# The last pair of output rows reordered, and the scaling of the causal pool put directly behind a reciprocal in both attentions

## The chip, the cores and the metric

The kernel runs on one core of a Trainium2 chip. The metric is the device time of one execution in microseconds (us). Five engines work side by side: TensorE (PE, with its weight load as PEld), VectorE (DVE), ScalarE (ACT), GpSimd (POOL) and SyncE (SP). Each runs its own instructions in the order in which they were written down for it; semaphores tie them together. In this kernel SP issues most of the DMAs, in its own order; a few are issued by ACT.

## The reference

One layer of a decoder trunk with 2048 positions and width 1024, all in float32:

```python
shift, scale, gate = split(silu(c) @ w_ada + b_ada)
u = x * (1 + scale) + shift
q, k, v, a_gate, p_in, p_gate, m_a, m_p = split(u @ w_in)
a = sliding_window_attention(q, k, v, sinks, bias) * silu(a_gate)     # window 128, 16 heads, 2 kv heads
a = a @ w_attn_proj
p = group_linear(causal_pool(p_in), w_pool_mix)                       # windows 2, 4, 8, 16
p = (p * pool_scale) * silu(p_gate)
p = p @ w_pool_proj
y = (sigmoid(m_a) * a + sigmoid(m_p) * p) @ w_out * (1 + gate)
x = layer_norm(alpha * x + y, ln_gain, ln_bias)
```

The causal pool of window w is the mean of the last w positions less the position itself. The part of it that the change touches is written in the kernel as `sum * (1/w) - value`, and then times the gate.

## The kernel before, in words

**Products.** Every product of two float32 blocks is made of three matmul passes over a high and a low half (`hi`, `lo`), so it stays accurate to float32. A block product of 256 rows by 1024 columns is a "quad" of a Strassen-like scheme: seven products, called B11, T1, T2, B21, T3, B22 and T4, of 12 matmuls of 128x512 each (`product`). Four of them are sums that several outputs share, so a few additions on DVE lie between them. In the profile an operand of a product is `set_B`, `set_T` or, in the last rows, `t4h`/`t4l`, its other operand is `w_set`; `mm` and `lg` are PSUM banks.

**Stages.** The sequence is worked in two halves of 1024 positions. For each half the gates are projected first, then the attention runs, and after both halves come the attention projection, the pool projection and the merge, and last `w_out` with the LayerNorm, in pairs of rows of 128 positions (`finish_pairs`, `out_quad`). The first attention takes from 256.3 to 584.8 us of the profiled execution, the second from 827.0 to 1157.8 us.

**An attention.** `attention` runs 67 iterations of about 4.9 us. An iteration issues, in this order, the scores of one block on PE (`lg<-kk,qs`), the transposes of an earlier block (`pt<-ident,L`), a reciprocal of sums on DVE (`sm<-sm`), then `close()`, the additions of the outputs `o` on DVE behind a copy on ACT (`o<-pv`), the scaling of probabilities `L<-L,sm` and the split of the transposed block (`pth` on ACT, `ptl` on DVE), the exponentials (`L<-L,nm` on ACT), five or six steps of three matmuls of other products (`filling`, 13 quads in all that have nothing to do with this block), the value matmuls (`pv<-pth,vv` and `pv<-ptl,vv`), and last `run_coming`, which runs whatever was queued for this iteration with `later`.

**What the fill products leave.** Their results go one of three ways. `take_p` makes the causal sums on POOL (`vb` to `nxt` to `fin`, as many additions as the window has powers of two), then, an iteration or two on, scales on DVE (`fin<-fin,...`), multiplies by the gate on POOL (`fin<-fin,pg`), and one iteration later sends the result to DRAM with a DMA on SP (`pin_B<-fin`). This happens 32 times, 16 in each half. `take_gate` copies a result to `raw` on ACT and sends it away with a DMA on SP (`ma_d<-raw`, `mp_d<-raw`); the tag `raw` has one buffer, so the next copy to it waits until the DMA before has landed. `seed` copies a bank on ACT (`mm<-mm`) that T2 of the next quad is accumulated onto. `split` prepares an operand: POOL adds the two blocks (`W<-W`), ACT casts the high half and POOL or DVE makes the low one (`w_set`); its blocks `W` and `A` are loaded by SP. In SP's order the loads of the next quad and the DMA of `raw` stand behind a `pin_B<-fin` at several places.

**`close()`.** The list `closing` holds additions `c + p5` of a quad (L948ff). It is emptied after the reciprocal of each iteration and ahead of T3 and T4.

**The last rows.** In `finish_pairs` a quad's T2, B21, T3, B22, T4 follow each other; T4 is accumulated onto the bank of T3 (`lg`). `consume` (L709) adds a product to the row held in `wide`, `last_stats` takes statistics of a half (L680), `last_norm` aggregates them (L685), adds epsilon (L686), makes the inverse root on POOL (L687, a power), multiplies by the gain (L688), and only when both rows 14 and 15 are done multiplies by the inverse root and adds the bias, by halves of 512 (L695), each followed by its DMA (L696). Most operations here are recorded with the line of a helper, L57.

The order in which `dve`, `pool`, `act`, `sp` and `pe` get their instructions is the program's own (`Ordered`); what is written with `nc.vector` may be moved by the scheduler.

Of the kernel before, what the change touches and what calls it, by code (L numbers as in the profile page):

```python
# [15 lines left out]
ALU = mybir.AluOpType  # L16
# [3 lines left out]
P = 128  # L20
D = 1024
S = 2048
KT = D // P
CH = 512
# [8 lines left out]
ALPHA = 2.0 ** 0.25  # L33
EPS = 1e-5
POOL_W = (2, 4, 8, 16)
# [25 lines left out]
def kernel(  # L61
# [22 lines left out]
    nc = tc.nc  # L84
# [15 lines left out]
    carry = cp.tile([P, KT, 16], F32, name="carry")  # L100
# [24 lines left out]
    def cols(t, n):  # L125
        return t[:, n * CH : (n + 1) * CH]
# [286 lines left out]
    def finish_pairs(ph, grp, opened, tick):  # L413

        lasts = []
        for q in grp:
            hi, lo = (ph.c(n, F32R) for n in ("t4h", "t4l"))
            nc.scalar.copy(hi, q.a22)
            low(nc.vector, lo, q.a22, hi)
            lasts.append((hi, lo))  # L420

        def begin(x):
            q, (a, b, _, _) = grp[x], opened[x]
            c, p5 = bank("lg"), ph.p("p5")
            nc.scalar.copy(c, a)
            nc.scalar.copy(p5, b)
            w = pair_split(ph, q.second())[::-1]
            q.late()
            return a, b, c, p5, w

        got = begin(0)
        for x, q in enumerate(grp):
            a, b, c, p5, w = got
            product(c, w[1], "T2")
            tick()
            w3 = pair_split(ph, q.third())[::-1]
            nc.vector.tensor_tensor(b, c, p5, ALU.add)
            product(a, w[0], "B21")
            tick()
            q.consume(ph, 0, 0, a)  # L440
            product(c, w3[1], "T3")
            tick()
            nc.vector.tensor_tensor(p5, c, p5, ALU.add)
            q.consume(ph, 1, 1, p5)
            product(b, w3[0], "B22")
            if x + 1 < len(grp):
                got = begin(x + 1)
            tick()
            q.consume(ph, 0, 1, b)
            product(c, lasts[x], "T4")  # L450
            tick()
            q.consume(ph, 1, 0, c)

# [189 lines left out]
    def norm_row(ph, row, z):  # L643
# [32 lines left out]
        for at, f in ((1, squares), (2, power), (3, scale), (3, store)):  # L676
            defer(at, f)

    def last_stats(row, n, zn):
        nc.vector.bn_stats(carry[:, row - 12, 6 * n : 6 * n + 6], zn)  # L680

    def last_norm(row, z):

        st, mv, rs = (carry[:, row - 12, a:b] for a, b in ((0, 12), (12, 14), (14, 15)))
        nc.vector.bn_aggr(mv, st)  # L685
        nc.vector.tensor_scalar(rs, mv[:, 1:2], EPS, None, ALU.add)  # L686
        nc.gpsimd.tensor_tensor(rs, rs, mhalf, ALU.pow)  # L687
        nc.vector.scalar_tensor_tensor(z, z, mv[:, 0:1], vec["gain"], ALU.subtract, ALU.mult)  # L688
        ending.append((row, z, rs))
        if row + 1 < S // P:  # L690
            return
        for row, z, rs in ending[::-1]:
            for n, q in enumerate((nc.sync, nc.scalar)):
                zn = cols(z, n)
                nc.vector.scalar_tensor_tensor(zn, zn, rs, cols(vec["lnb"], n), ALU.mult, ALU.add)  # L695
                q.dma_start(out[row * P : (row + 1) * P, n * CH : (n + 1) * CH], zn)  # L696

    ending = []

    def y_row(row):  # L700
        return y_d[row // 8, :, row // 4 % 2, :, row % 4 * P : (row % 4 + 1) * P].rearrange("k p q -> p k q")

    def out_quad(k):
        def consume(ph, mi, n, src):
            row = k + mi
            z, n_done = zs[row]
            zs[row][1] += 1
            zn = cols(z, n)
            nc.vector.scalar_tensor_tensor(zn, zn, ALPHA, src, ALU.mult, ALU.add)  # L709
# [66 lines left out]
    def attention(ph, s, fills, post, opened):  # L776
# [56 lines left out]
        def take_p(m, t, acc):  # L833
            n = max(now_n[0], pool_free[1] + 1, pool_free[0] + 3)
            pool_free[:] = pool_free[1], n
            wait = 1 if POOL_W[m // 2] < 8 else 2
            own = (m % 2, t) == (0, 1)
            x = []

            def first():  # L840
                x.append(ld("pg", gates_d["pg"][s, m, t], 2))
                x.extend(pool_sums(m, t, acc))

            def second():
                pg, p, copied = x
                dve.scalar_tensor_tensor(
                    p, p, 1.0 / POOL_W[m // 2], copied if own else acc, ALU.mult, ALU.subtract
                )
                pool.tensor_tensor(p, p, pg, ALU.mult)
                later(n + wait + 1, lambda: keep_raw(pin_d[s], m, t, p))  # L850

            later(n + wait, second)
            if own:
                free_b[0] = n
            if n == now_n[0]:
                first()
            else:
                later(n, first)
# [86 lines left out]
        closing = []  # L945

        def close():
            while closing:
                x, name = closing.pop()
                _, b, c, p5 = st[x]  # L950
                dve.tensor_tensor(b if name == "T2" else p5, c, p5, ALU.add)

        def filling():
            for i, (x, name) in enumerate(seq):
                begun(i)
                if name in ("T3", "T4"):
# [154 lines left out]
                sp.dma_start(as32(vv[:, 1 + NB :]), v_d[s, :, 1 + NB :])  # L1111
        for _ in fill:
            pass
        run_coming(True)
        result = []
        for x, q in enumerate(post):
# [558 lines left out]
```

## Time and profile before

| | |
|---|---|
| time, median of 3 runs (lowest to highest) | 1681.29 us (1681.26 to 1681.58) |
| profiled execution: its time | 1681.68 us |
| profiled execution: span of the core | 1679.9 us |
| DVE busy | 1208.6 us, 72% |
| ACT busy | 1026.3 us, 61% |
| POOL busy | 949.3 us, 57% |
| granted TensorE clock, mean | 0.997 |

The span is the time from the first to the last recorded instruction; 1.78 us of the profiled execution's own time lie outside it, and that execution took 0.39 us more than the median. In rows of a timeline the first number is the start in us, the second what it took in us, then engine, line, operation, `out<-in`, shape and a count; brackets at the end tell how long the engine had been idle and what ended that. A row of the engine SP tells when the DMA was issued, not when it landed. Several operations of one kind in a row are one row with a count.

### The profile page before, as it was taken

What the parts mean: (1) busy time and instruction counts of PE and PEld (TensorE: products, weight loads), DVE (VectorE), ACT (ScalarE), POOL (GpSimd) and SP (SyncE); (2) the same over time, 40 slices, a digit from 0 to 9 for tenths busy, and PEclk for the clock granted to TensorE, in tenths of its full rate; (3) what the DMA queues carried; (4) which work ended last, traced back from release to release, by engine and by line L of the source; (5) the groups of instructions that cost most, each with busy time, mean ns of one, the idle gap of its engine ahead of it and who ended that gap; (6) DMA issues with size and microseconds to landing.
All of it is one profiled execution on the core that took longest, in us unless ns stands there. A gap on an engine that the chain in (4) does not pass through costs nothing.

```text
span 1679.9 us, 24661 instructions
## 1 busy us (share of the span) xinstructions
PE 1642.9 (98%) x8058; PEld 1382.7 (82%) x8058; DVE 1208.6 (72%) x2156; ACT 1026.3 (61%) x2146; POOL 949.3 (57%) x710
## 2 busy tenths in 40 slices
PE   7999999999999999999999999999999999999997
PEld 6788888888888788888888888888878878878886
DVE  6955656676867867566467677777769896979777
ACT  4754547778778755334577777776647464554452
POOL 3343437585867838773376858597445453423442
PEclk9999999999999999999999999999999999999999
DMA  9688844343543578872432335345968896677443
GB/s 362 209 291 296 204 158 124 99 126 107 176 137 113 188 278 298 312 273 94 154 128 88 126 131 171 118 127 188 330 215 313 274 321 219 227 271 235 155 147 113
DMA packets 185971, 331.56 MB, mean 197 GB/s; under 512 B 18017, under 2 KB 43761, under 8 KB 185841
## 3 DMA queue, kind: packets, MB, share of 16 engines
q1 hardware_dynamic: 182720, 325.72, 56.8%
q10 hardware_dynamic: 3088, 4.23, 1.1%
q8 instruction: 64, 1.05, 0.3%
q14 instruction: 67, 0.54, 0.1%
q0 software_dynamic: 32, 0.02, 0.0%
HBM read 223.77 MB, written 109.28 MB: 198 GB/s over the span
## 4 chain that ended last, share of the span: by engine, by line
PE 80%; DVE 7%; DMA 5%; ACT 3%; issue 2%; POOL 2%; SPq 1%; POOLq 0%; DVEq 0%; ACTq 0%
PE mm L57 51%; PE lg L57 22%; PE pv L57 4%; PE pt L57 4%; DMA head_T<-in_wada_dram 1%; DMA g<-mp_d 1%; DVE w_set L132 1%; DVE L L57 1%; SPq L57 1%; DVE set_T L57 1%; DMA head_B<-in_wada_dram 1%; DVE room L57 1%; DVE w_set L57 0%; DMA g<-ma_d 0%; ACT g L609 0%
## 5 line engine op out<-in xcount | busy, mean ns | idle before, releaser
L57 PE MATMUL mm<-set_B,w_set 128*128 128x512 f32 x2664 | 652.6, 392 | 0.9 <-DVE w_set L57 0.4
L57 PEld LDWEIGHTS mm<-set_B,w_set 128*128 128x128 f32 x2664 | 495.8, 188 | 103.2 <-DVE w_set L57 0.8
L57 PE MATMUL mm<-set_T,w_set 128*128 128x512 f32 x1824 | 453.4, 395 | 2.1 <-DVE mm L57 1.2
L57 PE MATMUL lg<-set_T,w_set 128*128 128x512 f32 x1704 | 411.3, 391 | 7.6 <-ACT w_set L303 2.8
L57 PEld LDWEIGHTS mm<-set_T,w_set 128*128 128x128 f32 x1824 | 336.3, 188 | 70.8 <-DVE mm L57 4.2
L57 PEld LDWEIGHTS lg<-set_T,w_set 128*128 128x128 f32 x1704 | 319.6, 188 | 78.0 <-issue 3.7
L132 DVE TENSOR_TENSOR w_set<-W,w_set 128x1024 fp32r<-128x1024 f32 x137 | 192.5, 1405 | 142.3 <-ACT w_set L303 133.0
L303 ACT CAST w_set<-W 128x1024 fp32r<-128x1024 f32 x137 | 144.0, 1051 | 192.8 <-PE mm L57 148.3
L266 POOL TENSOR_TENSOR W<-W,A 128x512 f32<-128x512 f32 x46 | 73.5, 1598 | 271.6 <-DMA A<-in_win_dram 66.5
L57 POOL TENSOR_TENSOR w_set<-W,w_set 128x512 fp32r<-128x512 f32 x120 | 159.1, 1333 | 110.4 <-ACT w_set L57 108.6
L57 DVE TENSOR_TENSOR o<-pv,o 64x128 f32<-64x128 f32 x256 | 71.9, 281 | 96.8 <-ACT o L57 93.4
L57 POOL TENSOR_TENSOR W<-W 128x512 f32<-128x512 f32 x82 | 111.1, 1368 | 52.8 <-DVE sm L57 25.8
L57 ACT ACTIVATE L<-L,nm 128x257 f32<-128x257 f32 (+1 forms) x256 | 127.1, 498 | 17.8 <-DVE nm L57 8.2
L275 POOL TENSOR_TENSOR W<-W 128x512 f32<-128x512 f32 x46 | 71.9, 1563 | 103.9 <-DVE w_set L132 94.0
L270 POOL TENSOR_TENSOR W<-W 128x512 f32<-128x512 f32 x44 | 80.3, 1828 | 83.1 <-DVE w_set L132 66.7
L57 DVE CUSTOM_DVE_ANT_0 L<-lg,bt,nsink 128x256 f32<-128x256 f32 (+1 forms) x256 | 111.6, 473 | 15.2 <-DMA pg<-pg_d 10.8
L57 ACT CAST w_set<-W 128x512 fp32r<-128x512 f32 (+1 forms) x165 | 101.4, 628 | 24.4 <-POOL W L57 14.5
L57 ACT COPY o<-pv 64x256 f32<-64x256 f32 x128 | 47.3, 369 | 71.3 <-PE pv L57 70.1
L271 POOL TENSOR_TENSOR W<-W 128x512 f32<-128x512 f32 x44 | 69.1, 1570 | 32.4 <-DMA W<-in_win_dram 16.4
L57 ACT ACTIVATE L<-L,sm 128x256 f32<-128x256 f32 (+1 forms) x128 | 64.3, 502 | 36.6 <-DVE sm L57 36.2
L57 DVE TENSOR_TENSOR ptl<-pt,pth 128x512 fp32r<-128x512 f32 (+1 forms) x128 | 85.7, 669 | 1.0 <-ACT pth L57 0.9
L57 POOL TENSOR_TENSOR spare<-spare 128x512 f32<-128x512 f32 x48 | 80.2, 1679 | 8.1 <-ACT spare L57 6.0
(233 smaller groups left out, 2411.6 us busy)
## 6 DMA issues: line engine op xcount, KB each, us to landing
W<-in_win_dram SPq DMA_DIRECT2D x42, 512.0 KB, 5.8
W<-in_win_dram SPq DMA_DIRECT2D x42, 256.0 KB, 4.0
A<-in_win_dram SPq DMA_DIRECT2D x42, 256.0 KB, 4.9
ag_d<-sig SPq DMA_DIRECT2D x32, 256.0 KB, 5.9
pg_d<-sig SPq DMA_DIRECT2D x32, 256.0 KB, 4.4
pg<-pg_d SPq DMA_DIRECT2D x32, 256.0 KB, 3.2
pin_B<-fin SPq DMA_DIRECT2D x32, 256.0 KB, 2.0
ag<-ag_d SPq DMA_DIRECT2D x32, 256.0 KB, 3.1
```

Of the source, the lines that this page charges most:

```text
L57: return lambda *args, **kw: self.tc.keep_in_program_order(op(*args, **kw))
L132: engine.tensor_tensor(dst, src, as32(hi), ALU.subtract)
L266: e.tensor_tensor(self.w[:, 1, :], self.w[:, 2, :], self.a22, ALU.add)
L270: e.tensor_tensor(x[:, 1, :], x[:, 1, :], x[:, 0, :], ALU.subtract)
L271: e.tensor_tensor(x[:, 2, :], x[:, 0, :], x[:, 2, :], ALU.subtract)
L275: e.tensor_tensor(x[:, 3, :], x[:, 3, :], x[:, 1, :], ALU.subtract)
L303: a.copy(by_two(hi), raw)
```

## The change

**In the attentions.** `second` no longer scales and multiplies by itself in `run_coming`. It appends a function (`scaled`) to `closing`, which runs behind the next iteration's reciprocal, or ahead of T3 or T4 if that comes first. The additions `c + p5` now go into the same list, at its front. The DMA of the result stays queued for the same iteration as before.

**In the last pair.** For the last quad alone B22 is computed ahead of T3. T4 goes into the bank that B21 left, from nothing, in place of being accumulated onto T3's bank. The parts of the rows that are known early are added in place (`partly`), so that at the end a plain addition is left. The final scaling of a row is made of two functions (`last_halves`); the first half of row 14 is run ahead of T4, the rest after the last gain operation. The operations of the last two rows are kept in program order.

```diff
@@ finish_pairs
             q.consume(ph, 0, 0, a)
+            last = x + 1 == len(grp)
+            if last:
+                q.consume(ph, 1, 1, p5, True)
+                product(b, w3[0], "B22")
+                tick()
+                q.consume(ph, 0, 1, b)
             product(c, w3[1], "T3")
             tick()
-            nc.vector.tensor_tensor(p5, c, p5, ALU.add)
-            q.consume(ph, 1, 1, p5)
-            product(b, w3[0], "B22")
-            if x + 1 < len(grp):
+            if last:
+                q.consume(ph, 1, 1, c)
+                ending.pop(0)()
+                q.consume(ph, 1, 0, c, True)
+                c = a
+            else:
+                nc.vector.tensor_tensor(p5, c, p5, ALU.add)
+                q.consume(ph, 1, 1, p5)
+                product(b, w3[0], "B22")
                 got = begin(x + 1)
-            tick()
-            q.consume(ph, 0, 1, b)
-            product(c, lasts[x], "T4")
+                tick()
+                q.consume(ph, 0, 1, b)
+            product(c, lasts[x], "T4", last)
             tick()
             q.consume(ph, 1, 0, c)
@@ last_norm
+    def last_halves(row, z, rs):
+
+        def half(n, q):
+            zn = cols(z, n)
+            dve.scalar_tensor_tensor(zn, zn, rs, cols(vec["lnb"], n), ALU.mult, ALU.add)
+            q.dma_start(out[row * P : (row + 1) * P, n * CH : (n + 1) * CH], zn)
+
+        return [lambda n=n, q=q: half(n, q) for n, q in enumerate((nc.sync, nc.scalar))]
...
-        nc.vector.scalar_tensor_tensor(z, z, mv[:, 0:1], vec["gain"], ALU.subtract, ALU.mult)
-        ending.append((row, z, rs))
-        if row + 1 < S // P:
-            return
-        for row, z, rs in ending[::-1]:
-            for n, q in enumerate((nc.sync, nc.scalar)):
-                zn = cols(z, n)
-                nc.vector.scalar_tensor_tensor(zn, zn, rs, cols(vec["lnb"], n), ALU.mult, ALU.add)
-                q.dma_start(out[row * P : (row + 1) * P, n * CH : (n + 1) * CH], zn)
+        dve.scalar_tensor_tensor(z, z, mv[:, 0:1], vec["gain"], ALU.subtract, ALU.mult)
+        ending.extend(last_halves(row, z, rs))
+        if row + 1 == S // P:
+            for f in ending:
+                f()
@@ out_quad
+        begun = set()
+
+        def consume(ph, mi, n, src, partly=False):
...
+            if (row, n) in begun:
+                e.tensor_tensor(zn, src, zn, ALU.add)
+            else:
+                e.scalar_tensor_tensor(zn, zn, ALPHA, src, ALU.mult, ALU.add)
+            if partly:
+                begun.add((row, n))
+                return
@@ attention, take_p
             def second():
                 pg, p, copied = x
-                dve.scalar_tensor_tensor(
-                    p, p, 1.0 / POOL_W[m // 2], copied if own else acc, ALU.mult, ALU.subtract
-                )
-                pool.tensor_tensor(p, p, pg, ALU.mult)
+
+                def scaled():
+                    dve.scalar_tensor_tensor(
+                        p, p, 1.0 / POOL_W[m // 2], copied if own else acc, ALU.mult, ALU.subtract
+                    )
+                    pool.tensor_tensor(p, p, pg, ALU.mult)
+
+                closing.append(scaled)
                 later(n + wait + 1, lambda: keep_raw(pin_d[s], m, t, p))
@@ attention, close
         def close():
             while closing:
-                x, name = closing.pop()
-                _, b, c, p5 = st[x]
-                dve.tensor_tensor(b if name == "T2" else p5, c, p5, ALU.add)
+                closing.pop(0)()
+
+        def add_up(x, name):
+            _, b, c, p5 = st[x]
+            dve.tensor_tensor(b if name == "T2" else p5, c, p5, ALU.add)
...
-                        closing.append((x, name))
+                        closing.insert(0, lambda x=x, name=name: add_up(x, name))
```

The orders of SP and ACT are the same in both kernels, and PE's differs only in the last pair. POOL's and DVE's change at the 32 places of `take_p`. At 16 of them POOL's multiplication by the gate moves behind what followed it: at eight behind the multiplication of an output `o` by its gate, at two behind a sum `fin<-vb`, at two behind a `w_set`, and at four (the 10th and 14th of each attention, counted from 0) behind the whole set of sums of the next block.

The 14th place of the first attention, on POOL, before (`nxt` and the first `fin` are the sums of the next block, `fin_5779` is the block that is being finished, `pg` its gate, `W` and `w_set` operands of later products, `o` and `ag` an output of the attention and its gate):

```order
L57 TENSOR_TENSOR w_set_5917<-A22_5362,w_set_5917 128x512
L57 TENSOR_TENSOR fin_5779<-fin_5779,pg_5767 128x512
L57 TENSOR_TENSOR nxt_5939<-vb_5935 128x526
L57 TENSOR_TENSOR nxt_5941<-nxt_5939 128x524
L57 TENSOR_TENSOR nxt_5943<-nxt_5941 128x520
L57 TENSOR_TENSOR fin_5945<-nxt_5943 128x512
L57 TENSOR_TENSOR W_5695<-W_5695 128x512 x2
L57 TENSOR_TENSOR w_set_6045<-W_5695,w_set_6045 128x512
L57 TENSOR_TENSOR fin_5945<-fin_5945,pg_5933 128x512
L57 TENSOR_TENSOR o_5812<-o_5812,ag_5876 128x512
```

The same place on POOL now (numbers of the names shift by two):

```order
L57 TENSOR_TENSOR w_set_5917<-A22_5362,w_set_5917 128x512
L57 TENSOR_TENSOR nxt_5937<-vb_5933 128x526
L57 TENSOR_TENSOR nxt_5939<-nxt_5937 128x524
L57 TENSOR_TENSOR nxt_5941<-nxt_5939 128x520
L57 TENSOR_TENSOR fin_5943<-nxt_5941 128x512
L57 TENSOR_TENSOR fin_5779<-fin_5779,pg_5767 128x512
L57 TENSOR_TENSOR W_5695<-W_5695 128x512 x2
L57 TENSOR_TENSOR w_set_6045<-W_5695,w_set_6045 128x512
L57 TENSOR_TENSOR o_5812<-o_5812,ag_5876 128x512
L57 TENSOR_TENSOR fin_5943<-fin_5943,pg_5931 128x512
```

The multiplication `fin_5779<-fin_5779,pg_5767` now stands behind the four sums of the next block, and the next one (`fin_5943,pg`) behind `o_5812`.

SP around the DMA of that block, in the order that holds before and now (`pin0_B21<-fin_5779` is the row `pin_B<-fin` of the profile; `W` and `A22` are loads of a quad's blocks; `raw` is the result of another product):

```order
L57 DMA pg_5931<-pg_d_134 128x512
L57 DMA pin0_B21_120<-fin_5779 128x512
L57 DMA W_6040<-in_win_dram 128x512
L57 DMA A22_6041<-in_win_dram 128x512
L57 DMA W_6040<-in_win_dram 128x2x512
L57 DMA ma_d_135<-raw_6037 128x512
L57 DMA ain0_T1_102<-room1_5857 128x512
```

Nothing moved here: the DMA of `fin_5779` is ahead of three loads and of the DMA that empties `raw`.

DVE at the 15th place, shortly after, as one piece of the difference with the rows around it:

```order
 L57 TENSOR_TENSOR room0_5856<-room0_5856,room1_5857 128x512
-L57 SCALAR_TENSOR_TENSOR fin_5945<-fin_5945,p5_5491 128x512
 L57 RECIPROCAL sm_6026<-sm_6026 128x2
+L57 SCALAR_TENSOR_TENSOR fin_5943<-fin_5943,p5_5491 128x512
 L57 TENSOR_TENSOR o_6079<-pv_6060,o2_6080 64x128 x2
```

The reciprocal now stands ahead of the scaling, as at all 32 places.

DVE at the end of the program before (`wide4` is row 14, `wide5` row 15, `carry` the statistics, `wide0` and `wide1` the gain and the bias):

```order
L688 SCALAR_TENSOR_TENSOR wide4_16248<-wide4_16248,carry_73,wide0_15123 128x1024
L709 SCALAR_TENSOR_TENSOR wide5_16305<-wide5_16305,lg_16296 128x512
L695 SCALAR_TENSOR_TENSOR wide4_16248<-wide4_16248,carry_73,wide1_15125 128x512
L680 BN_STATS carry_73<-wide5_16305 128x6
L695 SCALAR_TENSOR_TENSOR wide4_16248<-wide4_16248,carry_73,wide1_15125 128x512
L685 BN_AGGR carry_73<-carry_73 128x2
L686 TENSOR_SCALAR carry_73<-carry_73 128x1
L688 SCALAR_TENSOR_TENSOR wide5_16305<-wide5_16305,carry_73,wide0_15123 128x1024
L695 SCALAR_TENSOR_TENSOR wide5_16305<-wide5_16305,carry_73,wide1_15125 128x512 x2
```

And now:

```order
L57 SCALAR_TENSOR_TENSOR wide4_16248<-wide4_16248,carry_73,wide0_15123 128x1024
L57 TENSOR_TENSOR wide5_16305<-lg_16296,wide5_16305 128x512
L57 BN_STATS carry_73<-wide5_16305 128x6
L57 SCALAR_TENSOR_TENSOR wide4_16248<-wide4_16248,carry_73,wide1_15125 128x512
L57 SCALAR_TENSOR_TENSOR wide5_16305<-wide5_16305,lg_16296 128x512
L57 TENSOR_TENSOR wide5_16305<-mm_16187,wide5_16305 128x512
L57 BN_STATS carry_73<-wide5_16305 128x6
L57 BN_AGGR carry_73<-carry_73 128x2
L57 TENSOR_SCALAR carry_73<-carry_73 128x1
L57 SCALAR_TENSOR_TENSOR wide5_16305<-wide5_16305,carry_73,wide0_15123 128x1024
L57 SCALAR_TENSOR_TENSOR wide4_16248<-wide4_16248,carry_73,wide1_15125 128x512
L57 SCALAR_TENSOR_TENSOR wide5_16305<-wide5_16305,carry_73,wide1_15125 128x512 x2
```

Before, both halves of row 14 were scaled around the statistics of row 15; now one half is, and the other follows row 15's gain operation. The first half of row 15 is completed by two operations, first from T3's bank (`lg`), then from T4's (`mm`), where it was one.

More of the change, by code (lines that the diff above doesn't have):

```diff
@@ L677, in norm_row @@
             defer(at, f)
+    ending = []
+    def last_halves(row, z, rs):
[4 more added lines that the diff above has]
+        return [lambda n=n, q=q: half(n, q) for n, q in enumerate((nc.sync, nc.scalar))]
     def last_stats(row, n, zn):
-        nc.vector.bn_stats(carry[:, row - 12, 6 * n : 6 * n + 6], zn)
+        dve.bn_stats(carry[:, row - 12, 6 * n : 6 * n + 6], zn)
     def last_norm(row, z):
         st, mv, rs = (carry[:, row - 12, a:b] for a, b in ((0, 12), (12, 14), (14, 15)))
-        nc.vector.bn_aggr(mv, st)
-        nc.vector.tensor_scalar(rs, mv[:, 1:2], EPS, None, ALU.add)
+        dve.bn_aggr(mv, st)
+        dve.tensor_scalar(rs, mv[:, 1:2], EPS, None, ALU.add)
         nc.gpsimd.tensor_tensor(rs, rs, mhalf, ALU.pow)
-        nc.vector.scalar_tensor_tensor(z, z, mv[:, 0:1], vec["gain"], ALU.subtract, ALU.mult)
-        ending.append((row, z, rs))
-        if row + 1 < S // P:
-            return
-        for row, z, rs in ending[::-1]:
-            for n, q in enumerate((nc.sync, nc.scalar)):
-                zn = cols(z, n)
-                nc.vector.scalar_tensor_tensor(zn, zn, rs, cols(vec["lnb"], n), ALU.mult, ALU.add)
-                q.dma_start(out[row * P : (row + 1) * P, n * CH : (n + 1) * CH], zn)
-    ending = []
+        dve.scalar_tensor_tensor(z, z, mv[:, 0:1], vec["gain"], ALU.subtract, ALU.mult)
[3 more added lines that the diff above has]
+                f()
     def y_row(row):
@@ L703, in out_quad @@
     def out_quad(k):
-        def consume(ph, mi, n, src):
+        begun = set()
+        def consume(ph, mi, n, src, partly=False):
             row = k + mi
             z, n_done = zs[row]
+            zn = cols(z, n)
+            e = dve if row > 13 else nc.vector
+            if (row, n) in begun:
[5 more added lines that the diff above has]
+                return
             zs[row][1] += 1
-            zn = cols(z, n)
-            nc.vector.scalar_tensor_tensor(zn, zn, ALPHA, src, ALU.mult, ALU.add)
             if row > 13:
@@ L1113, in attention @@
             pass
+        close()
         run_coming(True)
```

## The prediction

> **What bounds the kernel now.** I read the page's first part, then PE's waits, then the timelines of all engines around the places where POOL's order changes, and last the end of the program.
>
> ```profile
> PE 1642.9 (98%) x8058; PEld 1382.7 (82%) x8058; DVE 1208.6 (72%) x2156; ACT 1026.3 (61%) x2146; POOL 949.3 (57%) x710
> ...
> PE pv L57 <- ACT pth L57: 2.4, 4, 1.4
> ...
> PE pv L57 <- DVE ptl L57: 2.0, 5, 0.6
> ...
> PE mm L57 <- DVE sm L57: 0.9, 2, 0.4
> ...
> ACT w_set L57 <- POOL W L57: 14.5, 10, 4.3
> ```
>
> PE is busy 98% of the span, so time is won only where PE stands still, and lost wherever something makes it stand still. The rows of waits (us in all, times, the longest) are those of PE in an attention that DVE or ACT ends behind a reciprocal: 2.4 + 2.0 + 0.9 = 5.3 us in the whole program. That is the most that a better place for the reciprocal can give. ACT's longest waits behind those are for POOL's `W`, which is a sum of blocks for another product and not the scaling.
>
> **Why it can lose: a chain through SP and `raw`.** The place is the one shown in the part on the change, at 556 us. The rows are POOL's, SP's, ACT's, DVE's and PE's timelines, and the answer on the tile `raw` there.
>
> ```profile
> 556.54 1.74 POOL L57 TENSOR_TENSOR fin<-fin,pg 128x512 f32<-128x512 f32 x1
> 558.24 1.06 POOL L57 TENSOR_TENSOR nxt<-vb 128x526 f32<-128x526 f32 x1
> ...
> 563.44 1.29 POOL L57 TENSOR_TENSOR W<-W 128x512 f32<-128x512 f32 x1
> ...
> 558.31 0.32 SPq L57 DMA_DIRECT2D pin_B<-fin  x1
> 558.72 0.39 SPq L57 DMA_DIRECT2D W<-in_win_dram  x1
> ...
> 560.49 0.37 SPq L57 DMA_DIRECT2D ma_d<-raw  x1
> ...
> DMA to landing us min/median/max: 5.7/5.7/5.7
> ...
> 568.52 0.58 ACT L57 COPY raw<-mm 128x512 f32<-128x512 f32 x1
> ...
> 570.15 0.37 ACT L57 COPY o<-pv 64x256 f32<-64x256 f32 x1
> ...
> 572.13 0.68 DVE L57 TENSOR_TENSOR ptl<-pt,pth 128x512 fp32r<-128x512 f32 x1
> ...
> 573.15 0.40 PE L57 MATMUL pv<-ptl,vv 128*128 128x256 f32 x2
> ...
> 578.32 0.50 PE L57 MATMUL mm<-set_T,w_set 128*128 128x512 f32 x1 [0.43 <-DVE sm L57]
> ```
>
> The multiplication ends at 556.54 + 1.74 = 558.28, and SP issues `pin_B<-fin` at 558.31: SP was standing at it. The loads behind it follow at once, and so does `ma_d<-raw`, which lands at 560.49 + 5.7 = 566.19, 7.47 us after the first load was issued. ACT copies the next result to `raw` at 568.52. The landing is 2.33 us ahead of that copy, and this is all the slack there is, since `raw` has one buffer. Behind the copy on ACT stand the seed for the next T2, a `w_set`, the copy `o<-pv`, and then the probabilities and `pth`; DVE's `o` and `ptl` wait for those, and PE's value matmuls for `ptl`. `ptl` is done at 572.13 + 0.68 = 572.81 and PE uses it at 573.15: 0.34 us to spare.
>
> In the changed order the four sums run ahead of the multiplication, and SP's order is as it was. So SP's loads, the landing and the copy to `raw` come later by the sums' time.
>
> **What the sums take.** In the rows above the four sums lie between 558.24 and 563.44: 5.20 us. That includes slowing beside DVE, and the sums will now run 1.7 us earlier, beside other operations; the group of the last sums shows what one takes at its fastest and slowest.
>
> ```profile
> L57 POOL TENSOR_TENSOR fin<-nxt x24: 1038/1041/1834, 343.9 to 1134.6; 128x512 f32<-128x512 f32 x24
> ...
> 1130.73 1.51 POOL L57 TENSOR_TENSOR nxt<-vb 128x526 f32<-128x526 f32 x1
> ...
> 1136.39 1.29 POOL L57 TENSOR_TENSOR W<-W 128x512 f32<-128x512 f32 x1
> ...
> 1131.21 0.38 SPq L57 DMA_DIRECT2D W<-in_win_dram  x1
> ...
> 1134.69 0.33 SPq L57 DMA_DIRECT2D ma_d<-raw  x1
> ...
> DMA to landing us min/median/max: 3.2/3.2/3.2
> ...
> 1141.48 0.57 ACT L57 COPY raw<-mm 128x512 f32<-128x512 f32 x1
> ...
> 1145.11 0.69 DVE L57 TENSOR_TENSOR ptl<-pt,pth 128x512 fp32r<-128x512 f32 x1
> ...
> 1146.11 0.40 PE L57 MATMUL pv<-ptl,vv 128*128 128x256 f32 x2
> ```
>
> The least is four times 1.04 = 4.2 us, the most what stands there: 5.20, and in the second attention 1136.39 - 1130.73 = 5.66. From the first load to the landing of `raw` it took 7.47 us above and 1134.69 + 3.2 - 1131.21 = 6.68 here, where `raw` itself was late; both ends are kept. The loss of PE at a place is then: issue of the first load, plus the sums, plus 6.68 to 7.47, less the start of the next copy to `raw`, less PE's spare time at `ptl`.
>
> - First attention, 14th place: 558.72 + 4.2 + 6.68 - 568.52 = 1.08 to 558.72 + 5.20 + 7.47 - 568.52 = 2.87 us of delay; less 0.34 makes 0.74 to 2.53. PE's stall of 0.43 at 578.32, where it waits for a reciprocal, may take some of it back. I take the middle, 1.6.
> - Second attention, 14th place: 0.61 to 2.86 by the same sum. The spare time is 1146.11 - 1145.80 = 0.31. That leaves 0.30 to 2.55; I take 1.5, near the middle, since neither end is nearer.
>
> The 10th places have three sums, and more to spare:
>
> ```profile
> 452.19 1.50 POOL L57 TENSOR_TENSOR nxt<-vb 128x518 f32<-128x518 f32 x1
> ...
> 455.88 1.34 POOL L57 TENSOR_TENSOR W<-W 128x512 f32<-128x512 f32 x1
> ...
> 452.67 0.38 SPq L57 DMA_DIRECT2D W<-in_win_dram  x1
> ...
> 461.03 0.56 ACT L57 COPY raw<-mm 128x512 f32<-128x512 f32 x1
> ...
> 464.46 0.69 DVE L57 TENSOR_TENSOR ptl<-pt,pth 128x512 fp32r<-128x512 f32 x1
> ...
> 467.23 0.40 PE L57 MATMUL pv<-ptl,vv 128*128 128x256 f32 x2
> ...
> 1025.44 0.38 SPq L57 DMA_DIRECT2D W<-in_win_dram  x1
> ...
> 1033.80 0.56 ACT L57 COPY raw<-mm 128x512 f32<-128x512 f32 x1
> ...
> 1037.68 0.69 DVE L57 TENSOR_TENSOR ptl<-pt,pth 128x512 fp32r<-128x512 f32 x1
> ...
> 1040.22 0.40 PE L57 MATMUL pv<-ptl,vv 128*128 128x256 f32 x2
> ```
>
> Three sums take 3 x 1.04 = 3.1 to 455.88 - 452.19 = 3.69 us. The delay of the copy is 452.67 + 3.1 + 6.68 - 461.03 = 1.42 to 2.80 in the first attention, and 1.42 to 2.80 in the second. To spare are 467.23 - 465.15 = 2.08 and 1040.22 - 1038.37 = 1.85. The losses are 0 to 0.72 and 0 to 0.95; most of each range is at nothing, and I take 0.1 and 0.2.
>
> **The other places.** At 12 of the 32 the multiplication moves behind one operation of POOL of about 1.3 us (`o`, `w_set` or a last sum); SP is late by as much or less, under the slack of 2.33 us found above, which stands for them as the nearest row: I take nothing, and at the worst 0.5 us in all. At the other 16 POOL's order is the same. On DVE the reciprocal runs ahead of a scaling, so the scaling is late by one reciprocal and PE is reached sooner only where PE waits: at least 0, at most the 5.3 us above. I take nothing, since ACT's long waits in front of those stalls are for POOL's `W`, and `W` stands behind the same operations of POOL as before. If the sums should run at their fastest, `W` comes about 1 us sooner at two places, so 0.9 us is a fair bound for what is won.
>
> **The tail.**
>
> ```profile
> 1672.58 0.73 DVE L695 SCALAR_TENSOR_TENSOR wide<-wide,carry,wide 128x512 f32<-128x512 f32 x1
> ...
> 1675.25 1.41 DVE L695 SCALAR_TENSOR_TENSOR wide<-wide,carry,wide 128x512 f32<-128x512 f32 x2 [0.44 <-POOL carry L687]
> ...
> 1644.64 0.55 POOL L57 TENSOR_TENSOR rs<-rs,mhalf 128x1 f32<-128x1 f32 x1
> 1673.70 1.52 POOL L687 TENSOR_TENSOR carry<-carry,mhalf 128x1 f32<-128x1 f32 x1 [2.50 <-DVE carry L686]
> ```
>
> The last product is the last work of PE before and now, so the tail is worth only what follows it on DVE. Before row 15's aggregate one half of row 14 goes away (0.73 at most); behind its gain one half comes back, of which 0.44 us falls into the wait for POOL's power. That is -0.44 at best. Row 15 has one addition more, about as long as a half, and if DVE is late at the end of T4 it costs 0.7: +0.3. The power takes 0.55 us alone and 1.52 beside DVE's gain operation; now a second operation of DVE follows the gain at once, so either it or the power is held up, at most 0.55. The tail lies between -0.4 and +0.8; I take 0, the price of no change in its nearest row.
>
> The Trainium skill ("SBUF — State Buffer", section "SBUF: two separate sides") says that VectorE with two SBUF inputs and GpSimd exclude each other on a shared port pair for a whole instruction, whoever comes first. By that rule the moved half and the power cannot overlap, and the tail would come out at about +0.3; without it at about -0.2. The two power rows, 0.55 and 1.52, agree with it.
>
> **The sum.** 1.6 + 1.5 + 0.1 + 0.2 + 0 = +3.4 us. On the profiled execution (span 1679.9, with 1.78 us outside it, 1681.68) it gives 1685.1; that execution was 0.39 above the median of 1681.29, so on the median's footing it is **1684.7 us**. With both ends of each place it is +0.6 to +6.8, hence 1681.9 to 1688.1; that all ends fall together is unlikely, and this case's own range is 1682.3 to 1687.2.
>
> **Rivals.**
>
> - The transfers are hidden: SP does not hold the loads back, or `raw` lands as soon after its issue as the 3.2 us of the second attention (560.49 + 5.20 + 3.2 = 568.89 against 568.52, a delay of 0.37, equal to the spare time). For it speaks that landing; against it that the 5.7 belongs to the case in which `ma_d` follows the loads at once, which is what happens in the changed order. Time: 1681.3, with the tail 1680.9 to 1681.9. The Trainium skill ("DMA: Bandwidth & Descriptors", section "Anatomy of one DMA — SWDGE (gpsimd) path") says that a semaphore wait is spent on the issuing sequencer and the DMA engines do not wait. By it the loads stay behind `pin_B` and this rival falls; `pin_B` at 0.03 us behind its multiplication agrees.
> - Faster: DVE's reciprocal, no longer behind a scaling that waits for POOL, frees ACT and PE sooner. The price is up to the 5.3 us of PE's waits, and 0.9 by the bound above; it decides only if `raw` lands before 568.52 and 1141.48, so that none of the +3.4 is paid. For over 0.2% it must win 3.4 of the 5.3. Time: 1680.4, at best 1677.
> - Worse: every end at its high value, or a late seed that also stalls the next products and their casts. Time: 1687 to 1688.5.
> - The tail alone decides, through the shared port: at most +0.8, 1682.1; it falls in with the first.
>
> **How the numbers follow.** What a measurement of this kernel can tell from no change is about 0.2%, 3.36 us: 1677.9 to 1684.65. Chances: the chain through SP and `raw` 0.62, hidden 0.22, faster engines 0.08, worse 0.08. The bound of slower lies at the middle of the likeliest case, so this gives 0.36 to slower and 0.26 to same; worse adds 0.08 to slower, hidden 0.22 to same, and of the faster engines 0.04 pass the bound. Faster 0.04, same 0.52, slower 0.44. The range takes in the likeliest and most of the hidden: 1680.9 to 1687.2.
>
> **What would show it.** In the changed profile, at the 14th place of each attention: `pin_B<-fin` issued some 5 us later than before, `ma_d<-raw` landing at about 570.9 and 1143.5, ACT's copy to `raw` waiting for that DMA, and PE's `pv<-ptl` held by `ptl` some 1.5 us. Right in size if the two attentions are longer by about 1.7 us each. In the tail the last DMA is issued within half a microsecond of before, counted from T4's end. I am wrong if the copy to `raw` does not wait (then the landing was priced wrongly), or if it waits and PE does not (then ACT and DVE had more to spare than `ptl` shows), or if PE's waits for `pth` and `ptl` shrink all over the attentions.

## The result and the profile after

The changed kernel took 1685.19 us (median of 10 runs, 1683.5 to 1686.42), the kernel before 1680.61 in the same comparison (10 runs, 1679.51 to 1682.11). The ratio is 1.0026 with a 95% interval of 1.0018 to 1.0034: slower by 4.6 us, by the medians. Here and below a ratio is estimated from all the runs of both kernels, so it need not equal the quotient of the two medians. The profiled execution of the changed kernel has a span of 1683.8 us, 3.9 more than before.

First the page of the changed kernel and its waits (for PE and for ACT: us in all, times, the longest).

```profile
PE 1645.1 (98%) x8058; PEld 1382.9 (82%) x8058; DVE 1210.8 (72%) x2157; ACT 1025.5 (61%) x2146; POOL 949.8 (56%) x710
...
PE mm L57 <- ACT mm L57: 5.0, 4, 1.4
...
PE pv L57 <- DVE ptl L57: 3.3, 8, 0.6
...
PE pv L57 <- ACT pth L57: 1.3, 4, 0.5
...
ACT raw L57 <- DMA ma_d<-raw: 12.9, 6, 3.1
```

The row `PE mm <- ACT mm` is new; the waits before had none like it. PE waits four times, 5.0 us in all, for ACT's `mm`, the seed copy. ACT in turn waits 12.9 us for the DMA that empties `raw`, 11.4 of them at the four places of the prediction. The waits for `pth` have gone from 2.4 to 1.3 us, those for `ptl` from 2.0 to 3.3.

The chain at the 14th place of the first attention, from the timelines of POOL, SP, ACT and PE and the answer on the tile `raw`:

```profile
556.78 1.52 POOL L57 TENSOR_TENSOR nxt<-vb 128x526 f32<-128x526 f32 x1
...
562.25 1.34 POOL L57 TENSOR_TENSOR fin<-fin,pg 128x512 f32<-128x512 f32 x1
563.54 1.74 POOL L57 TENSOR_TENSOR W<-W 128x512 f32<-128x512 f32 x1
...
563.61 0.32 SPq L57 DMA_DIRECT2D pin_B<-fin  x1
564.02 0.38 SPq L57 DMA_DIRECT2D W<-in_win_dram  x1
...
565.60 0.55 SPq L57 DMA_DIRECT2D ma_d<-raw  x1
...
DMA to landing us min/median/max: 6.2/6.2/6.2
...
571.92 0.59 ACT L57 COPY raw<-mm 128x512 f32<-128x512 f32 x1 [2.74 <-DMA ma_d<-raw]
572.40 0.59 ACT L57 COPY mm<-mm 128x512 f32<-128x512 f32 x1
...
573.05 2.34 PE L57 MATMUL mm<-set_T,w_set 128*128 128x512 f32 x9 [1.44 <-ACT mm L57]
...
576.13 0.51 PE L57 MATMUL pv<-ptl,vv 128*128 128x256 f32 x2 [0.51 <-DVE ptl L57]
```

The sums take 562.25 - 556.78 = 5.47 us, the multiplication follows them, and `pin_B` is issued 0.02 us after it ends (563.59). The first load is issued at 564.02, 5.30 us later than before, and `raw` lands at 571.8, 7.8 after it. ACT has waited 2.74 us for that, the seed is late, and PE stands 1.44 us at the product that needs the seed and 0.51 at `ptl`.

The 10th place of the first attention, SP, ACT and PE:

```profile
456.14 0.38 SPq L57 DMA_DIRECT2D W<-in_win_dram  x1
...
457.71 0.56 SPq L57 DMA_DIRECT2D ma_d<-raw  x1
...
463.96 0.59 ACT L57 COPY raw<-mm 128x512 f32<-128x512 f32 x1 [3.06 <-DMA ma_d<-raw]
...
462.78 0.94 PE L57 MATMUL mm<-set_T,w_set 128*128 128x512 f32 x3
465.09 3.01 PE L57 MATMUL mm<-set_T,w_set 128*128 128x512 f32 x12 [1.36 <-ACT mm L57]
```

The same chain, and here PE stands 1.36 us where the sum had 0.1. In the second attention ACT waited 3.08 and 2.54 us for `raw` at the two places, and PE 0.97 and 1.23 for the seed.

### The profile page after: what moved, and what is told of

Read it like the earlier page. It is cut to its first block, busy times and chain, and to the rows that moved or that the text cites. A ratio compares the mean times of both kernels' runs of the same rounds, so it can differ in the third digit from the quotient of the medians.

```text
span 1683.8 us, 24664 instructions
## 1 busy us (share of the span) xinstructions
PE 1645.1 (98%) x8058; PEld 1382.9 (82%) x8058; DVE 1210.8 (72%) x2157; ACT 1025.5 (61%) x2146; POOL 949.8 (56%) x710
## 4 chain that ended last, share of the span: by engine, by line
PE 76%; DVE 7%; POOL 5%; ACT 5%; DMA 4%; issue 3%; SPq 0%; DVEq 0%; POOLq 0%; ACTq 0%
PE mm L57 47%; PE lg L57 22%; PE pv L57 3%; PE pt L57 3%; DMA ma_d<-raw 1%; POOL nxt L57 1%; ACT L L57 1%; POOL W L57 1%; ACT w_set L57 1%; POOL fin L57 1%; DVE w_set L57 1%; DVE wide L57 1%; DVE w_set L132 1%; POOL w_set L57 1%; DVE set_T L57 1%
```

## The experiments

"Attention 1" and "2" are the lengths in the trace from the start of the first score matmul (`lg<-kk,qs`) to that of the last; the tail is from the end of the last matmul to the end of the span. Each row of times has the kernel before in the same comparison beside it.

| kernel | median us | before | ratio, 95% interval | attention 1 | attention 2 | tail |
|---|---|---|---|---|---|---|
| before | | | | 328.49 | 330.78 | 9.46 |
| the change | 1685.19 | 1680.61 | 1.0026, 1.0018 to 1.0034 | 331.63 | 333.37 | 9.33 |
| tail only | 1680.42 | 1681.04 | 0.9996, 0.9987 to 1.0005 | 329.18 | 330.81 | 9.34 |
| attentions only | 1684.95 | 1681.04 | 1.0022, 1.0013 to 1.0031 | 331.23 | 333.32 | 9.46 |
| POOL's order only | 1685.41 | 1681.04 | 1.0025, 1.0016 to 1.0033 | 330.89 | 333.17 | 9.45 |
| sums behind | 1679.78 | 1681.04 | 0.9989, 0.9980 to 0.9998 | 328.32 | 330.54 | 9.33 |
| change, raw sent by ACT | 1684.47 | 1680.82 | 1.0019, 1.0010 to 1.0027 | 329.42 | 332.83 | 9.34 |
| before, raw sent by ACT | 1681.61 | 1680.82 | 1.0004, 0.9995 to 1.0013 | 328.65 | 330.94 | 9.46 |
| 10th places late | 1682.53 | 1680.82 | 1.0014, 1.0005 to 1.0023 | 329.65 | 331.75 | 9.33 |
| 14th places late | 1682.91 | 1680.82 | 1.0013, 1.0005 to 1.0022 | 330.17 | 332.24 | 9.33 |
| change, loads behind raw | 1679.43 | 1680.86 | 0.9995, 0.9986 to 1.0003 | 328.19 | 330.41 | 9.35 |
| before, loads behind raw | 1680.59 | 1680.86 | 0.9999, 0.9990 to 1.0008 | 328.59 | 330.78 | 9.46 |
| both cures | 1679.86 | 1680.86 | 0.9995, 0.9987 to 1.0004 | 328.38 | 330.62 | 9.34 |

**One part of the change at a time.** The first kernel has the change's `finish_pairs`, `last_halves` and `consume` and the attentions of before; the second has the reverse.

> The attentions are those of before, the last pair is that of the change. Chain theory (POOL's multiplication behind the sums holds SP, the DMA of raw lands late, ACT's copy to raw and the seed behind it hold PE): the tail has no part in it, so -0.5 to +0.5 us against before, and from T4's end to the span's end 9.3 us as in the changed kernel (9.46 before). Rival that the tail brings the loss through VectorE's and GpSimd's shared port: +3 to +5 us here.

> The last pair is that of before, the attentions are those of the change. Chain theory: the whole of the loss, +4.0 to +5.2 us against before, with PE waiting for ACT's mm at four places for about 1.0 to 1.5 us each. Rival that the tail brings it: within 1 us of before.

The tail only: 0.9996, with the tail 0.12 us shorter. The attentions only: 1.0022, and the attentions as long as the change's to within 0.4 us. All of the loss that can be told lies in the attentions. By the medians the two are -0.6 and +3.9 us against before; each lies about 0.1 us outside what had been expected, far less than its interval is wide.

**POOL's order or DVE's.** In the kernel before, one line of `second` changed, so that DVE scales where it did and only POOL's multiplication is written later:

```diff
                 dve.scalar_tensor_tensor(
                     p, p, 1.0 / POOL_W[m // 2], copied if own else acc, ALU.mult, ALU.subtract
                 )
-                pool.tensor_tensor(p, p, pg, ALU.mult)
+                closing.append(lambda: pool.tensor_tensor(p, p, pg, ALU.mult))
```

> Before, with one thing changed: POOL's multiplication by the gate is written where the change has it, behind the next sums; VectorE's order is that of before, and so is the last pair. Chain theory: POOL's order alone makes the loss, +3.5 to +5.2 us, and the four waits of PE for ACT's mm are there. Rival that VectorE's order (the scaling behind the reciprocal) makes it: within 0.5 us of before and none of the four waits.

And in the changed kernel the next block's sums moved behind the waiting multiplication, so that POOL has its old order there and DVE keeps its new one (`pool_sums` makes its copies to `vb` as before and returns its additions as a function; `waiting` tells that a scaling stands in `closing`):

```diff
-                x.extend(pool_sums(m, t, acc))
+                sums = pool_sums(m, t, acc)
+                if waiting:
+                    closing.append(lambda: x.extend(sums()))
+                else:
+                    x.extend(sums())
```

> The change, with the next block's sums written behind the waiting multiplication, so that POOL has the order of before at the four places with three or four sums (and at the two with one); VectorE's order stays that of the change, the multiplication stays behind an o or a w_set at the ten other places. Chain theory: the four waits of PE for ACT's mm are gone, and the time is that of before, -1.5 to +0.8 us. Rival that the scaling behind the reciprocal costs by itself, or that the delay of SP by one operation at the other places is enough: +3 us or more stay.

POOL's order alone: 1.0025, the whole loss. The sums behind: 0.9989, nothing left of it. PE's and ACT's waits of the two, first POOL's order only:

```profile
PE pv L57 <- ACT pth L57: 2.9, 4, 1.8
...
PE mm L57 <- ACT mm L57: 2.0, 3, 1.6
...
ACT raw L57 <- DMA ma_d<-raw: 11.8, 6, 2.9
```

Then the sums behind:

```profile
PE pv L57 <- DVE ptl L57: 2.5, 6, 0.6
...
PE pv L57 <- ACT pth L57: 1.4, 4, 0.5
...
ACT raw L57 <- DMA ma_d<-raw: 1.5, 2, 0.9
```

In the second there is no wait of PE for ACT's `mm`, and ACT's for `raw` have gone from 11.8 to 1.5 us. In the first the wait for the seed is 2.0 us in three places and not four of 1.0 to 1.5, as had been expected. The row of `pth`, 2.9 us, is not where the rest went, since the kernel before has most of that wait too, ahead of the late `raw`:

```profile
566.85 0.51 PE L57 MATMUL pv<-pth,vv 128*128 128x256 f32 x2 [1.40 <-ACT pth L57]
```

With POOL's order only, the same wait, the stage behind it, and the seed's wait at the 10th place of the first attention (PEclk is the granted clock, 1 at its most):

```profile
568.11 0.50 PE L57 MATMUL pv<-pth,vv 128*128 128x256 f32 x2 [1.83 <-ACT pth L57]
...
core 0: us, PE busy (x) PEld busy (x) DVE busy (x) ACT busy (x) POOL busy (x), PEclk, DMA share, GB/s
570.40:573.80 3.40, 3.40 (x10) 2.32 (x9) 1.20 (x2) 1.65 (x4) 3.32 (x3) 0.50 0.95 361
...
464.96 0.50 PE L57 MATMUL mm<-set_T,w_set 128*128 128x512 f32 x1 [0.30 <-ACT mm L57]
```

At the 14th place of the first attention the granted clock of this execution was 0.50 for 3.4 us. PE came over a microsecond later to the product that needs the seed and had no wait for it left, though ACT had waited 2.25 us for `raw`; that the wait is missing there is no sign that `raw` was in time. At the 10th places PE waited 0.30 and 0.15 us for the seed, where the change has 1.36 and 0.97; `raw` landed 7.2 and 7.4 us after the first load there in place of 7.74 and 7.75, and ACT waited 2.52 and 2.72 us in place of 3.06 and 3.08. So what the 10th places cost hangs on DVE's order too, in a way that was not looked into. Over the attentions as a whole POOL's order makes the loss: they are as long as the change's to within 0.8 us, and the time is as long.

**What of the late multiplication holds PE: `raw`, or the loads.** SP issues both late. In the first pair of kernels the DMA of `raw` is issued by ACT, directly behind the copy, in the changed kernel and, as a control, in the one before:

```diff
                 act.copy(x, src)
-            later(now_n[0], lambda: sp.dma_start(gates_d[name][s, m, t], x))
+            (later(now_n[0], lambda: sp.dma_start(gates_d[name][s, m, t], x)) if kept else act.dma_start(gates_d[name][s, m, t], x))
```

> The change, with the DMAs that empty raw issued by ACT directly behind the copy, so that they no longer stand behind pin_B and the loads in SP's order; POOL's, DVE's and SP's orders are otherwise those of the change. Theory that the late landing of raw is what holds ACT and PE: the copies to raw wait no more at the four places, PE's waits for ACT's mm go, and the time falls from the change's +4.6 to -1.5 to +1.5 us against before (ACT pays about 30 issues and has to wait for its own copy to end at each). Rival that the late loads of W and A behind the multiplication hold PE by themselves: +3 us or more stay, with PE waiting for w_set at these places.

> Control of the run before: the same edit in the kernel before, where the DMA of raw is not late. Theory: no gain to be had from it, -0.5 to +1.5 us against before, which is what ACT pays. If the edit alone were worth as much as it is worth in the changed kernel (-3 to -4.6 us), the run before would tell nothing of the change.

The control: 1.0004. The change: 1.0019, where my theory had expected it near 1. ACT's timeline at the 10th place shows why:

```profile
461.75 0.56 ACT L57 COPY raw<-mm 128x512 f32<-128x512 f32 x1
464.55 0.33 ACTq L57 DMA_DIRECT2D ma_d<-raw  x1
464.92 0.57 ACT L57 COPY mm<-mm 128x512 f32<-128x512 f32 x1 [2.61 <-DMA W<-in_win_dram]
```

The copy to `raw` waits no more, at none of the four places. But now the issue of the DMA waits, for 2.2 us behind the end of the copy, and the profile puts the idle time behind it down to the landing of the load `W`. The trace also names the semaphore of each DMA: those of SP and ACT share eight, and this one has the semaphore of the 512 KB load of `W`, which SP issued at 458.39 and which landed at 464.47. The issue stood at three of the four places (464.55, 1038.84 and 1145.96 against copies begun at 461.75, 1035.50 and 1144.43), each time until the load of `W` with its semaphore had landed (464.47, 1038.48 and 1145.89). At the fourth the load with its semaphore, one of `A`, had landed at 568.05; the DMA was issued at 570.12, directly behind the copy of 569.51, and attention 1 got most of its time back. So the run put a new wait in the place of the old one and by itself decides neither way.

The second pair takes the other side: SP keeps the DMA of `raw`, and the loads are queued behind it.

```diff
                 if x < K:
-                    quads[x + 1].load(ph, False, sp, None)
+                    later(now_n[0], lambda: quads[x + 1].load(ph, False, sp, None))
```

> The change, with the loads of the next quad queued for the end of the iteration, so that in SP's order they stand behind the DMA that empties raw in place of ahead of it; POOL, ACT, DVE and PE keep the change's orders. SP still stands at pin_B until the multiplication, and the loads come a little later than in the change. Theory that the late landing of raw (7.5 us behind the first load) is what holds ACT and PE: raw lands 2 to 4 us after the multiplication, the four copies to raw wait for nothing, and the time is -1.5 to +1.0 us against before. Rival that the late loads hold PE: +3.5 us or more.

> Control: the same order of SP in the kernel before. Theory: raw was not late there, so nothing is won, -0.8 to +0.8 us against before. A gain of 3 us here would mean that the edit is worth that much whatever POOL's order.

The change with the loads behind: 0.9995; the control 0.9999. POOL's multiplication and `pin_B` come behind the sums as in the change, `pin_B` at 562.85 where it was at 558.31 before, and the first load follows it after 0.9 us in place of 0.4; and the loss is gone. SP and ACT at the 14th place, and the landing:

```profile
562.85 0.32 SPq L57 DMA_DIRECT2D pin_B<-fin  x1
563.26 0.38 SPq L57 DMA_DIRECT2D ma_d<-raw  x1
563.74 0.40 SPq L57 DMA_DIRECT2D W<-in_win_dram  x1
...
DMA to landing us min/median/max: 2.5/2.5/2.5
...
568.31 0.57 ACT L57 COPY raw<-mm 128x512 f32<-128x512 f32 x1
```

`raw` lands 2.5 us after its issue, in place of 6.2, at 565.8, and the copy at 568.31 waits for nothing. The late loads of `W` and `A` cost PE nothing that can be seen; what cost was that `raw` stood behind them.

**Both cures together.**

> The change with both cures, the next block's sums behind the multiplication and the loads behind the DMA of raw. Theory: the two cures take away the same wait, so together they are worth no more than the first alone, which measured 0.9989 of before: -2.0 to -0.3 us. If the loss had two causes, this would be faster than that by a microsecond or more.

0.9995: no more than either alone, as it has to be if both take away one and the same wait.

**How much each place costs.** The kernel with the sums behind, but for one kind of place: `if waiting and POOL_W[m // 2] != 8` leaves the 10th places as in the change, `!= 16` the 14th.

> Sums behind the multiplication everywhere but at the 10th places of both attentions, so only those two (three sums each) are as in the change. By the prediction's term +0.3 us over the kernel with all sums behind. By the changed trace, in which PE waits 1.36 and 0.97 us for ACT's mm there: +1.9 to +2.7 over it, that is +0.6 to +1.6 against before.

> The same with only the 14th places (four sums each) as in the change. By the prediction's terms +3.1 us over the kernel with all sums behind; by the attentions' lengths in the traces, less what the 10th places show, +3.0 to +3.6 over it, that is +1.7 to +2.5 against before.

The times of the two, 1.0014 and 1.0013, have intervals that overlap too far to tell them apart. By the medians they are +1.7 us, 0.1 above what was expected, and +2.1. The attentions' lengths tell them apart. Against the kernel with all sums behind, the 10th places add 1.33 and 1.21 us, the 14th 1.85 and 1.70; together 6.1, and the change itself is 3.31 + 2.83 = 6.1 longer than that kernel. The places add up.

## Why the prediction was right, point by point

**The mechanism** stands as it was put up to ACT's copy: the sums ahead of the multiplication, SP standing at `pin_B`, the loads and the DMA of `raw` behind it, one buffer of `raw`, ACT's wait. Taking back POOL's order at the places with sums removes the loss, making POOL's order alone makes it, and letting `raw` pass the loads removes it too. The last link was another than the prediction's. It had PE held at `ptl` for some 1.5 us; PE was held at the product that needs the seed, 1.44 and 1.23 us at the 14th places, and then 0.51 at `ptl`. A late seed stood in the prediction only under the rival "worse", at 0.08.

**The size.** 1684.7 was forecast and 1685.19 measured; against the kernel before that is +3.4 forecast and +4.6 measured. That the two times lie within 0.5 us is in part luck: the forecast stood on a median of 1681.29 for the kernel before, and that kernel took 1680.61 in the comparison. The chances leaned the other way, 0.52 for the same and 0.44 for slower; by the prediction's own bound of 3.36 us the kernel came out slower. The forecast of the four places was 1.6 + 1.5 + 0.1 + 0.2 = 3.4 us of PE; the attentions of the trace show 1.85 + 1.70 + 1.33 + 1.21 = 6.1, and the two attentions are 3.1 and 2.6 us longer than before, not 1.7 each. Both kinds of place were sized wrongly, the 10th places most. Two of the prediction's sums are also uneven: "+0.6 to +6.8" takes in the tail's low end and not its high one, with which it is +7.6; and 5.3 us won from 1681.29 would be 1676, not 1677.

- The 10th places, forecast at 0.1 and 0.2 from ranges that ended at 0.72 and 0.95, cost 1.33 and 1.21. The price of a landing was taken between 6.68 and 7.47 us after the first load, and the lower end did not belong: it came from places where `raw` itself was late, so that the DMA did not stand behind the loads alone. At the four places of the changed kernel it took 7.82, 7.62, 7.74 and 7.75 us. With 7.75 and the sums' 3.69 the 10th places come to 452.67 + 3.69 + 7.75 - 461.03 = 3.08 us of ACT's wait, and 3.06 was measured. (Counted from the attention's start, the first load came 4.2 us later, not 3.69, and ACT itself came to the copy 0.6 later; the two cancel.) With DVE's old order these places cost much less, as shown above. The spare time that I took from `ptl`, 2.08, was 1.7: it was the seed that PE came to first, not `ptl`, and of 3.06 us it was spared 3.06 - 1.36.
- At the 14th places the middle of the range was taken for the same reason, 1.6 and 1.5 for 1.85 and 1.70. PE waited there at the seed first (1.44) and only then at `ptl` (0.51), where the prediction had `ptl` alone.
- The other places were taken at nothing, under a slack of 2.33 us that was to stand for them all. At two of them there was no such slack: ACT's copies at 381.74 and 957.29 waited 0.89 and 0.62 us for `raw`. PE had no wait for it there, so nothing stands as their price.

**What took some of it back.** The kernel with the sums behind has attentions shorter than those of before by 0.17 and 0.24 us and a tail shorter by 0.13. The other profiles agree: the three kernels with DVE's new order and without the loss have 328.19 to 328.38 and 330.41 to 330.62 us, the four with the attentions of before or its controls 328.49 to 329.18 and 330.78 to 330.94. (The 329.18 of the tail only holds a stretch at clock 0.50, from 568.5 to 571.9; without it the first range ends at 328.65.) That is some 0.3 us in each attention, where I had taken nothing and bounded it at 0.9 in all. It is argued, not shown, that the reciprocal's new place wins it: the three kernels also have POOL's multiplication behind one operation at ten or more places, and where DVE's order alone differs, between POOL's order only and the attentions only, the attentions with the new order are 0.34 and 0.15 us longer, with `raw` late in both kernels. The sums behind, at 0.9989, have an interval that ends at 0.9998; both cures together came out at 0.9995 with an interval that takes in 1, so a gain over the kernel before is not certain.

**What stays open.** From the 6.1 us the 0.4 of the attentions and the tail's 0.1 go off, which makes 5.6; the spans differ by 3.9 and the medians by 4.6. In the profiled executions the changed kernel's stretch between the last score matmul and the last matmul is 1.2 us shorter than before, 511.5 for 512.7, and its first attention begins 0.7 us earlier. But with the old code the profiled executions of before and of its two controls show 512.7, 513.0 and 510.0 for that stretch, so this is how much it varies from one execution to the next. Much of that spread goes with the clock: in that stretch the execution with 513.0 has two pieces of 3.4 us at clock 0.50, that with 512.7 one, and that with 510.0 none. The changed kernel has one as well, so its 1.2 us are not explained by it, and I draw nothing from them.

**The tail** was taken at 0, between -0.4 and +0.8, and came out at -0.13 in the change; all profiled kernels with the new tail have 9.33 to 9.35 us there, all with the old one 9.46 or 9.45. The last operations of DVE and POOL:

```profile
1677.43 1.52 POOL L709 TENSOR_TENSOR carry<-carry,mhalf 128x1 f32<-128x1 f32 x1 [4.21 <-DVE carry L57]
...
1677.27 3.27 DVE L57 SCALAR_TENSOR_TENSOR wide<-wide,carry,wide 128x1024 f32<-128x1024 f32 x4
```

The gain operation and the three halves now follow each other on DVE with no gap, where before DVE had waited 0.44 us for the power. The moved half of row 14 needs only row 14's power, and stands where DVE waited for row 15's. The prediction's +0.3 did not come. It was drawn from a rule of the Trainium skill ("SBUF — State Buffer", section "SBUF: two separate sides"), that VectorE with two SBUF inputs and GpSimd exclude each other for a whole instruction. The power's 1.52 us beside the gain operation fits that rule; the half behind it does not:

```profile
1678.46 0.75 DVE L57 SCALAR_TENSOR_TENSOR wide<-wide,carry,wide 128x512 f32<-128x512 f32 x1
```

The power's row lasts from 1677.43 to 1678.95, as long as before, and the half from 1678.46 to 1679.21, as long as the two after it. By these rows, of which POOL's are rough, the two overlap for 0.5 us and neither is held up.

**The rivals.** That the transfers are hidden was refuted by ACT's waits of 2.5 to 3.1 us for `raw`. That faster engines would win: the waits for `pth` fell by 1.1 us, those for `ptl` rose by 1.3. Held against the first rival was the Trainium skill's rule that a semaphore wait is spent on the issuing sequencer ("DMA: Bandwidth & Descriptors", section "Anatomy of one DMA — SWDGE (gpsimd) path"); that section is about GpSimd's DMAs, and SP's agree with it here: 0.02 us from the multiplication's end to `pin_B` at the 14th place, and the loads behind it.

## What to carry to other kernels

When an operation moves on one engine, ask which DMA waits for its result and what stands behind that DMA in its issuer's order; the cost may come out ten microseconds later on an engine that shares nothing with the operation but that queue. A DMA that frees a single buffer should not be queued behind large loads, least of all behind a store that waits for a late producer. And when a transfer's time is priced from the profile, take it from a place where the same transfers stood ahead of it, and look at the first instruction that needs the result, not at the best known one.

## What was not expected of the hardware

- The time of a 256 KB store was set by the loads issued just ahead of it on the same queue: 2.4 to 2.5 us from issue to landing when it went first, 6.0 to 6.2 in the change, where it went behind loads of 256, 256 and 512 KB.
- A DMA moved to ACT's queue did not leave the others behind: its issue stood 2.2 us behind the end of its copy, until the load of SP's queue that has the same semaphore had landed, and ACT's own work stood with it.
- The granted clock fell to 0.50 for 3.4 us in some executions and not in others: in the first attention from 568.5 in the tail only and from 570.4 in POOL's order only, in no attention of the other kernels, and once between 1513 and 1518 in six of the thirteen profiled executions. What brings it on was not looked into. A single trace can so hide a wait, or add to a stage what the code did not.
